# Bias rows behind V's weights and in the attention, SyncE in a fixed order until V is back, down's residual stores one per weight unit

## The chip, the cores and the metric

The kernel runs on one core of a Trainium2 chip. The metric is the device time of one execution in microseconds (us); the time of a kernel is the median over several runs. The core has five engines that work side by side, each in its own program order: PE (TensorE, matrix products), DVE (VectorE), ACT (ScalarE), POOL (GpSimd) and SP (SyncE, which here only issues transfers). Transfers (DMAs) are issued by SP and in some places by ACT; sixteen DMA engines carry them out.

## The reference, cut to what matters

The computation is a transformer encoder of two layers over 1024 tokens of 1024 features, in fp32. Each layer has a combined input projection, three groups of attention heads (A: neighbourhood attention on a grid, with a relative bias; B: a sliding window with a T5 bias and sinks; C: dense, with norms and rotary), an output projection, and a SwiGLU FFN of width 2816.

```python
def reference(x, c, w_mod, b_mod, g_attn, w_in, rpb_na, sink_sw, t5_table, gq_ax, gk_ax,
              g_group, w_o, g_ffn, w_gu, w_down, g_final):
    cond = jax.nn.silu(c)
    for l in range(DEPTH):
        mod = cond @ w_mod[l] + b_mod[l]
        sh_a, sc_a, gt_a, sh_f, sc_f, gt_f = [m[:, None, :] for m in split_cols(mod, (D,) * 6)]
        h = rms_norm(x, g_attn[l]) * (1 + sc_a) + sh_a
        proj = h @ w_in[l]
        qa, ka, va, qb, kb, vb, qc, kc, vc = split_cols(proj, IN_SPLITS)
        ya = neighborhood_attention(qa, ka, va, rpb_na[l])
        yb = sliding_window_attention(qb, kb, vb, sink_sw[l], t5_table)
        yc = axial_attention(qc, kc, vc, gq_ax[l], gk_ax[l])
        y = jnp.concatenate([rms_norm(ya, ga), rms_norm(yb, gb), rms_norm(yc, gc)], axis=-1)
        x = x + gt_a * (y @ w_o[l])
        h = rms_norm(x, g_ffn[l]) * (1 + sc_f) + sh_f
        gate, up = split_cols(h @ w_gu[l], (FFN_HIDDEN, FFN_HIDDEN))
        x = x + gt_f * ((jax.nn.silu(gate) * up) @ w_down[l])
    return rms_norm(x, g_final)
```

## The kernel before

Every fp32 operand of a product is held as two rounded halves, hi and lo, and each product is three matmuls (hi x hi, hi x lo, lo x hi) with 512 columns, accumulated in PSUM. So every weight block that arrives by DMA passes two steps before PE can use it: ACT rounds it (`whi<-wst`, `wpt<-w`, `wpt<-graw`), and DVE or POOL subtracts to get the rest (`wlo<-wst,whi`).

All instructions are issued through one helper, so the profile puts them all on line L49; they are told apart by their tiles. The helper can pin an engine: `pin(engines, True)` ties each further instruction of that engine to the one before it in program order, without a wait. Where an engine isn't pinned, a scheduler places its instructions by its own costs, and may move a transfer far from where the code has it. A transfer, whether issued by SP or by ACT, takes the next of eight completion semaphores (DMAHW0 to DMAHW7) in turn, and its issue waits until the transfer that had the same semaphore before has landed.

A layer runs through these stages, in the order of PE:

1. Token projections: a loop t = 0 to 9 over blocks of 128 tokens. It makes group C's queries and keys (norm, rotary on POOL and DVE: `cq`, `ct`; transposes `pq`, `pk`), a first part of the queries and keys of A and B (`ps_ab`, rounded to `qko` and stored to DRAM as `qkd` by SP), and at t = 8 and 9 the first V products (`ps_v`). `v_stage` at t = 4 loads V's weights as four pairs of 128 rows (tiles `wst`, `wst`, `wsv`, `wsv`, three transfers each). In layer 0 `bias_rows` at t = 3 makes the bias tables in DRAM: `skA` (two, one for each layer, each 4 x 128 copies of a row of 512 values, 1 MB, DRAM to DRAM), `rowB` (the T5 bias less its mask, 12 KB) and `skB` (six, each 128 copies of a row of `rowB`, 256 KB). The tables for group A of layer 0, `zv<-skA`, read the first skA in stage 2; layer 1 reads the second. `bz<-skB` reads skB in the attention, for group B.
2. The AB stage: the other V products (`v_proj`), then the queries and keys of A and B by columns `oc` 2 to 7 in two halves each, twelve halves of 24 matmuls (`ps_ab`). After each half ACT and DVE round the result (`qko`) and ACT issues two stores `qkd<-qko`, one half later. Beside this SP streams the adaLN weights (`wmt`), which DVE multiplies and adds up (`acc`), and loads the AB weights (`wst`).
3. The heads' attention: a stream n of pairs, 24 of C, 16 of A and 24 of B, with scores (`sC`), ACT's exponential (`pr`), transposes (`T`, `pt`) and products with V (`pv`). At n = 0 eight `v_store` write A's part of V to DRAM (`vAd<-vs`) and at n = 6 eight `v_back` bring it back in another order of rows (`vs<-vAd`), 256 KB each.
4. The output projection, then the FFN: gate and up, whose result goes to DRAM (`gpd`), and down, 77 weight units of 48 matmuls in seven products in the order 1, 2, 6, 7, 4, 5, 3, with weights `w` and activations `graw<-gpd` (one transfer for two units) loaded ahead. In layer 0, when product 4 is done, the gains and rotary tables of the next layer are loaded (`g`, `cst`), and `spill(0)` stores the finished half of the residual in eight transfers (`xd<-xb`).

SP is pinned in stage 2 and in the FFN, and unpinned in stages 1 and 3. So the vAd stores and vs loads, which the code issues in the attention, are placed by the scheduler: it has moved them up into the AB stage, among the wmt.

## Time and profile before

| what | us |
|---|---|
| median of 3 runs | 2412.68 (2412.14 to 2415.06) |
| profiled execution | 2419.0 |
| its span | 2417.2 |
| PE busy | 2343.7 (97% of the span) |
| DVE busy | 1756.8 (73%) |
| ACT busy | 1194.7 (49%) |
| POOL busy | 744.0 (31%) |

In the rows of the timeline a line gives the start and duration in us, the engine, the operation with its output and input tiles, the shape, and in brackets how long the engine stood idle before it and what it waited for. `SPq` and `ACTq` are the issues of transfers by SP and ACT; their duration is the time to issue, and with several in one row it takes in the waits between them. "DMA to landing" is the time from the issue to the arrival of the last byte. PEclk is the share of TensorE's full clock that was granted.

### The profile page before, as it was taken

The page shows a single profiled execution, that of the slowest core. Times are in us where ns is not written, and L with a number is a line of the kernel's source. Part 1 is how long each engine was busy: PE and PEld are TensorE (multiplying, and loading weights), DVE is VectorE, ACT ScalarE, POOL GpSimd, SP SyncE. Part 2 cuts the span into 40 slices and gives each one's busy share as a digit, 9 for nine tenths or more (in the row PEclk, how much of TensorE's full clock was granted, in tenths as well). Part 3 has the DMA queues.
Part 4 walks back from the last instruction along what each step waited for, and adds up shares of the span by engine and source line. Part 5 has one row for each costly group of instructions (what it writes and reads, how often), then busy time and mean ns, then how long its engine had stood idle before and what let it go on. Part 6 is the DMA issues. An engine that isn't in the chain of part 4 may idle for free.

```text
span 2417.2 us, 33362 instructions
## 1 busy us (share of the span) xinstructions
PE 2343.7 (97%) x11733; PEld 1957.8 (81%) x11733; DVE 1756.8 (73%) x2788; ACT 1194.7 (49%) x2250; POOL 744.0 (31%) x719
## 2 busy tenths in 40 slices
PE   8999999999999999999999999999999999999998
PEld 4777899888788787788787879988888888888886
DVE  5756898977967788587578579988797545447865
ACT  3421688954543333344444138897454333334443
POOL 1430345720144444300037114465004444430001
PEclk9999999999999999999999999999999999999999
DMA  8478215254245454596433861151534332329633
GB/s 264 143 235 274 71 27 133 58 178 149 92 144 179 157 182 153 158 285 191 138 110 97 282 198 32 27 161 61 196 99 160 116 101 96 121 90 298 212 129 109
DMA packets 305336, 356.95 MB, mean 148 GB/s; under 512 B 51964, under 2 KB 221788, under 8 KB 305168
## 3 DMA queue, kind: packets, MB, share of 16 engines
q1 hardware_dynamic: 283296, 342.07, 44.5%
q10 hardware_dynamic: 21504, 12.59, 2.0%
q8 instruction: 92, 1.51, 0.2%
q14 instruction: 76, 0.62, 0.1%
q0 software_dynamic: 368, 0.17, 0.0%
HBM read 269.79 MB, written 88.63 MB: 148 GB/s over the span
## 4 chain that ended last, share of the span: by engine, by line
PE 45%; DVE 5%; issue 4%; DMA 4%; ACT 3%; POOL 1%; SPq 0%; ACTq 0%; POOLq 0%; DVEq 0%
PE ps_w L49 21%; PE ps_d L49 11%; PE ps_o L49 3%; PE pv L49 2%; PE T L49 2%; PE ps_v L49 2%; PE sC L49 2%; DMA qkd<-qko 1%; DVE wpt L49 1%; ACT pr L49 1%; DMA w<-in_w_down_dram 1%; PE ps_c L49 1%; DMA cst<-const_rope_dram 1%; DMA graw<-gpd 1%; DVE xb L49 0%
## 5 line engine op out<-in xcount | busy, mean ns | idle before, releaser
L49 PE MATMUL ps_d<-wpt 128*128 128x512 f32 x1848 | 424.3, 390 | 4.0 <-ACT wpt L49 3.4
L49 PEld LDWEIGHTS ps_d<-wpt 128*128 128x128 f32 x1848 | 345.5, 188 | 78.1 <-issue 3.3
L49 POOL TENSOR_SCALAR pr<-pr,rs 128x1024 f32<-128x1024 f32 (+2 forms) x248 | 193.7, 794 | 219.3 <-DVE rs L49 190.3
L49 POOL TENSOR_TENSOR sg<-sg,u 128x512 f32<-128x512 f32 x82 | 116.5, 1421 | 353.6 <-ACT sg L49 227.8
L49 PE MATMUL pv<-pt,vs 128*128 128x256 f32 x1088 | 175.5, 296 | 17.2 <-DVE y L49 13.3
L49 DVE TENSOR_TENSOR pt<-T,pt 128x512 fp32r<-128x512 f32 x272 | 176.8, 678 | 7.4 <-ACT pt L49 7.1
L49 ACT CAST wpt<-w 128x512 fp32r<-128x512 f32 x154 | 95.9, 622 | 170.5 <-PE ps_d L49 153.1
L49 ACT CAST pt<-T 128x512 fp32r<-128x512 f32 x272 | 152.3, 585 | 40.7 <-PE T L49 38.6
L49 ACT COPY u<-ps_w 128x512 f32<-128x512 f32 x128 | 75.2, 587 | 189.9 <-PE ps_w L49 189.9
L49 POOL TENSOR_TENSOR wpt<-ws,wpt 128x512 fp32r<-128x512 f32 x80 | 110.4, 1381 | 186.2 <-ACT wpt L49 139.8
L49 DVE TENSOR_TENSOR wpt<-w,wpt 128x512 fp32r<-128x512 f32 x154 | 109.4, 710 | 79.5 <-ACT wpt L49 79.3
L49 PEld LDWEIGHTS pv<-pt,vs 128*128 128x128 f32 x1088 | 141.4, 189 | 30.0 <-DVE y L49 25.6
L49 PE MATMUL T<-identr,pr 128*128 128x128 f32 x1176 | 161.6, 273 | 0.9 <-DVE edge L49 0.4
L49 DVE SCALAR_TENSOR_TENSOR acc<-wmt,condT,acc 128x512 f32<-128x512 f32 (+1 forms) x98 | 117.2, 1204 | 47.0 <-DMA wmt<-in_w_mod_dram 46.3
L49 PEld LDWEIGHTS T<-identr,pr 128*128 128x128 f32 x1176 | 137.9, 140 | 16.1 <-issue 1.4
L49 ACT CAST wpt<-ws 128x512 fp32r<-128x512 f32 x176 | 108.1, 624 | 59.8 <-issue 28.2
L49 DVE TENSOR_TENSOR wpt<-ws,wpt 128x512 fp32r<-128x512 f32 x96 | 81.8, 861 | 62.1 <-ACT wpt L49 62.0
L49 DVE TENSOR_TENSOR wpt<-graw,wpt 128x512 fp32r<-128x512 f32 x154 | 110.3, 716 | 21.3 <-ACT wpt L49 21.1
L49 ACT CAST wpt<-graw 128x512 fp32r<-128x512 f32 x154 | 95.2, 618 | 60.0 <-DMA graw<-gpd 50.5
L49 DVE TENSOR_REDUCE rs<-sC 128x1 f32<-128x1024 f32 x88 | 107.3, 1221 | 17.8 <-PE sC L49 13.7
L49 DVE TENSOR_TENSOR ws<-wr 128x512 f32<-128x512 f32 x88 | 78.9, 899 | 54.2 <-POOL wpt L49 51.1
L49 PE MATMUL sC<-qk 128*128 128x512 f32 x384 | 108.9, 407 | 6.4 <-ACT pr L49 6.4
(300 smaller groups left out, 5945.7 us busy)
## 6 DMA issues: line engine op xcount, KB each, us to landing
wr<-in_w_gu_dram SPq DMA_DIRECT2D x92, 512.0 KB, 4.2
gpd<-sg SPq DMA_DIRECT2D x154, 256.0 KB, 4.4
graw<-gpd SPq DMA_DIRECT2D x76, 512.0 KB, 3.5
w<-in_w_down_dram SPq DMA_DIRECT2D x110, 256.0 KB, 5.1
wmt<-in_w_mod_dram SPq DMA_DIRECT2D x48, 512.0 KB, 6.1
qk<-qkd SPq DMA_DIRECT2D x44, 512.0 KB, 6.6
wst<-in_w_o_dram SPq DMA_DIRECT2D x32, 512.0 KB, 3.9
wmt<-in_w_mod_dram SPq DMA_DIRECT2D x64, 256.0 KB, 3.7
```

What stands on the lines that cost most here:

```text
L49: ins = op(*args, **kwargs)
```

## The change

Three edits, all to what SP issues. The rows of PE, DVE, ACT and POOL are the same before and after.

The first splits `bias_rows`. The store of `rowB` stays at t = 3; the copy to layer 0's skA is written behind `v_stage` at t = 4, and the copy to layer 1's skA and the six skB are written at n = 4 of the attention, in layer 0. SP's rows in stage 1, from the first stores of `qkd` to V's weights, before (skA_92 is layer 1's table, skr the rows it copies):

```order
L49 DMA qkd<-qko 512x1x64 x4
L49 DMA skA_92<-skr 512x1x512
L49 DMA rowB<-wsv 6x512
L49 DMA qkd<-qko 512x1x64 x2
L49 DMA skB<-rowB 128x512 x6
L49 DMA qkd<-qko 512x1x64 x2
L49 DMA wst<-in_w_in_dram 128x2x256
L49 DMA wst<-in_w_in_dram 128x2x128 x2
L49 DMA wst<-in_w_in_dram 128x2x256
L49 DMA wst<-in_w_in_dram 128x2x128 x2
```

and after:

```order
L49 DMA qkd<-qko 512x1x64 x5
L49 DMA rowB<-wsv 6x512
L49 DMA qkd<-qko 512x1x64 x3
L49 DMA wst<-in_w_in_dram 128x2x256
L49 DMA wst<-in_w_in_dram 128x2x128 x2
L49 DMA wst<-in_w_in_dram 128x2x256
L49 DMA wst<-in_w_in_dram 128x2x128 x2
```

skA_92 and the six skB are gone from here, and V's weights follow the eight stores directly. Layer 0's own table, skA_91, stands further up in SP's rows, at the start of stage 1, where the scheduler places it in both kernels (these rows are of after; before has the same five):

```order
L49 DMA cst<-const_rope_dram 128x128 x4
L49 DMA t_428<-in_t_table_dram 32x6
L49 DMA skA_91<-skr 512x1x512
L49 DMA wst<-in_w_in_dram 128x8x128
L49 DMA xd<-xt 128x512 x16
```

Moved in the code, it has not moved on SP.

The second keeps SP pinned from the AB stage on until `v_back` at n = 6, in both layers, so that the order of the code holds there. SP's rows in the middle of layer 0's AB stage, before:

```order
L49 DMA wmt<-in_w_mod_dram 128x1024
L49 DMA wst<-in_w_in_dram 128x8x128
L49 DMA wmt<-in_w_mod_dram 128x1024 x2
L49 DMA zAd<-zt 128x640
L49 DMA wmt<-in_w_mod_dram 128x1024
L49 DMA vs<-vAd 128x1x512
L49 DMA wst<-in_w_in_dram 128x8x128
L49 DMA vs<-vAd 128x1x512 x4
L49 DMA wmt<-in_w_mod_dram 128x1024 x3
L49 DMA vs<-vAd 128x1x512 x3
L49 DMA wst<-in_w_in_dram 128x8x128
L49 DMA wmt<-in_w_mod_dram 128x1024 x6
```

and after, from the last weights of the AB stage to the attention:

```order
L49 DMA wmt<-in_w_mod_dram 128x1024 x3
L49 DMA wst<-in_w_in_dram 128x8x128
L49 DMA wmt<-in_w_mod_dram 128x1024 x6
L49 DMA vAd<-vs 128x512 x8
L49 DMA skA_92<-skr 512x1x512
L49 DMA skB<-rowB 128x512 x6
L49 DMA vs<-vAd 128x1x512 x8
L49 DMA qk<-qkd 64x2x1024 x2
L49 DMA qk<-qkd 128x1024
L49 DMA zA<-zAd 128x640 x2
L49 DMA bz<-skB 128x384 x2
L49 DMA wst<-in_w_o_dram 128x1024 x2
```

The eight vAd stores, which stood among the wmt in rows above the ones shown, and the eight vs loads now follow the last wmt, with skA_92 and the six skB between them. Behind these come the loads of the attention (qk, zA, bz) and of the output projection. Before, zA x2, bz x2 and two loads of w_o followed the last wmt directly, and then qk.

The third replaces `spill(0)` after product 4 of down in layer 0, eight stores in one go, by one store with each of the next eight units (`at_unit`). SP's rows there (cst are rotary tables), before:

```order
L49 DMA g_10827<-in_gq_ax_dram 128x6x64
L49 DMA g_10827<-in_gk_ax_dram 128x2x64
L49 DMA cst<-const_rope_dram 128x128 x4
L49 DMA xd<-xb 128x512 x8
L49 DMA graw<-gpd 128x1024 x2
L49 DMA cst<-const_rope_dram 128x128
L49 DMA graw<-gpd 128x1024 x3
L49 DMA xd<-xb 128x512 x4
L49 DMA graw<-gpd 128x1024 x2
```

and after:

```order
L49 DMA g_10827<-in_gq_ax_dram 128x6x64
L49 DMA g_10827<-in_gk_ax_dram 128x2x64
L49 DMA cst<-const_rope_dram 128x128 x4
L49 DMA xd<-xb 128x512 x2
L49 DMA graw<-gpd 128x1024
L49 DMA xd<-xb 128x512 x2
L49 DMA cst<-const_rope_dram 128x128
L49 DMA graw<-gpd 128x1024
L49 DMA xd<-xb 128x512 x2
L49 DMA graw<-gpd 128x1024
L49 DMA xd<-xb 128x512 x2
L49 DMA graw<-gpd 128x1024 x2
```

The stores now stand in twos between the loads of graw.

The diff:

```diff
--- before.py
+++ after.py
@@ -964,9 +964,12 @@
             for i in range(2):
                 pe.matmul(ps[0:6], t5h[:, i, :], oneh, start=(i == 0), stop=(i == 1))
             dve.tensor_tensor(out=mB, in0=mB, in1=ps[0:6], op=ALU.subtract)
-            for i in range(2):
-                sp.dma_start(skA[i], bc(skr[4 * i : 4 * i + 4][:, None, :], [4, P, 512]))
             sp.dma_start(rowB, mB)
+
+        def rows_A(i):
+            sp.dma_start(skA[i], bc(skr[4 * i : 4 * i + 4][:, None, :], [4, P, 512]))
+
+        def rows_B():
             for h in range(6):
                 sp.dma_start(skB[h], bc(rowB[h][None, :], [P, 512]))
 
@@ -1021,6 +1024,8 @@
                 w = split_tile(wab.pop(0), KC, (ct, "wx", 2))
                 for kp in range(4):
                     v_stage(kp)
+                if l == 0:
+                    rows_A(0)
             if t == 6:
                 v_split_w(pool)
                 v_split_w(dve)
@@ -1196,7 +1201,7 @@
                     mod_one()
                 store = ab_split(oc, half, ps, ab)
         store(act)
-        pin((pe, act, dve, sp, pool), False)
+        pin((pe, act, dve, pool), False)
         close(ab_cm)
         close(h_cm)
         close(ps_cm)
@@ -1645,6 +1650,11 @@
             if n in (0, 6):
                 for j in range(8):
                     (v_back if n else v_store)(j)
+            if n == 4 and l == 0:
+                rows_A(1)
+                rows_B()
+            if n == 6:
+                pin((sp,), False)
             if n == 50:
                 yq = qk_tile()
             if n == 54:
@@ -2273,7 +2283,8 @@
                     cc_cm, ccp = open_pool("cc", side="right")
                     csts.clear()
                     g8 = gains_load(ccp, 1)
-                    spill(0)
+                    for n in range(KC):
+                        at_unit(u + 1 + n, lambda n=n: spill(0, (n,)))
                 beside = chain(early_half(), odd_squares())
         for _ in beside:
             pass
```

## Prediction

> **What bounds the kernel.** I read the page first, then PE's waits, then the timeline of each engine around every PE wait that lies beside moved work.

> The page's busy time by engine:

> ```profile
> PE 2343.7 (97%) x11733; PEld 1957.8 (81%) x11733; DVE 1756.8 (73%) x2788; ACT 1194.7 (49%) x2250; POOL 744.0 (31%) x719
> ```

> The waits of PE, whole run (waited in total, times, longest):

> ```profile
> PE pv L49 <- DVE y L49: 13.3, 22, 1.0
> ...
> PE ps_d L49 <- ACT wpt L49: 3.4, 2, 2.6
> ...
> PE ps_v L49 <- POOL wlo L49: 1.7, 1, 1.7
> ...
> PE ps_ab L49 <- ACT whi L49: 1.6, 1, 1.6
> ...
> PE ps_ab L49 <- DVE wlo L49: 0.8, 1, 0.8
> ```

> PE is the bound, and its program order is the same in both kernels, as are DVE's, ACT's and POOL's; SP's alone differs. So the time can move only through PE's gaps, and through the clock that a gap can cost. Of 73.5 us outside PE's busy time most is work of other places (the 22 waits for y, for one) that no moved transfer touches. The last four rows lie beside moved transfers, and so does the start of attention; each is now followed to its cause.

> **Gap 1: layer 0, V's weights.** PE, then two windows (busy of PE, PEld, DVE, ACT, POOL; PEclk, DMA share, GB/s), then SP's issues, then ACT and POOL:

> ```profile
> 132.31 0.51 PE L49 MATMUL ps_v<-wlo,hh 128*128 128x512 f32 x1 [1.70 <-POOL wlo L49]
> 132.40:136.20 3.80, 3.80 (x10) 2.99 (x11) 3.80 (x5) 3.42 (x7) 0.00 (x0) 0.55 0.41 89
> 113.00:116.30 3.30, 3.30 (x22) 2.72 (x20) 2.46 (x5) 1.07 (x5) 3.30 (x2) 1.00 0.27 94
> 103.42 0.66 SPq L49 DMA_DIRECT2D skA<-skr  x1
> 107.65 2.86 SPq L49 DMA_DIRECT2D qkd<-qko  x2
> 116.33 3.76 SPq L49 DMA_DIRECT2D skB<-rowB  x6
> 121.46 5.23 SPq L49 DMA_DIRECT2D wst<-in_w_in_dram  x6
> 128.77 1.05 ACT L49 CAST whi<-wst 128x1024 fp32r<-128x1024 f32 x1 [4.44 <-DMA wst<-in_w_in_dram]
> 116.93 3.19 POOL L49 TENSOR_TENSOR ct<-cq,cst 128x512 f32<-128x512 f32 x3
> 125.20 1.35 POOL L49 TENSOR_TENSOR ct<-ct,ct 128x512 f32<-128x512 f32 x1
> 129.90 2.36 POOL L49 TENSOR_TENSOR wlo<-wst,whi 128x1024 fp32r<-128x1024 f32 x1 [3.35 <-DMA wsv<-in_w_in_dram]
> ```

> SP stops from 110.5 to 116.33 for the rows' store, then issues six copies of 256 KB, and only at 121.46 V's weights. ACT converts them at 128.77, POOL subtracts at 129.90, PE stands 1.70 us, and afterwards runs 3.80 us at a granted clock of 0.55: ten matmuls where a full clock would do some seventeen, 0.45 x 3.80 = 1.7 us. The gap costs 3.4 us, not 1.70. [...]

> The change takes the second large copy (the skA row) and the six skB out of this place. skA's other copy stands in the same SP row before and after, so moving it in the source is worth nothing. V's weights then issue from about 110.5, and with the 7.3 us that passed from 121.46 to ACT's start the first pair is in by 118. POOL ends its ct at 126.55 and adds 2.36: wlo at 128.9, against 130.6 when PE wanted it. The second pair's buffer is freed by the POOL work that ends at 116.93, so the rest issues by some 122.5 (5.23 for six) and is in by 129.8, still ahead of PE's need of it. I take the whole 3.4 (ends 0 and 3.4), with 1.7 us to spare. A later weight load, which waits for POOL too, now stands ahead of eight stores qkd in SP's rows; it waits for that same subtraction, so the stores follow from 129 on, and what reads them back belongs to the attention (sC first at 248.66, below): nothing.

> **Gap 2: layer 0, the AB stage.** PE, a window behind, ACT, SP; then how long the stores qkd took to land in two stretches (190 to 216, and 1410 to 1440):

> ```profile
> 226.29 0.51 PE L49 MATMUL ps_ab<-hh,whi 128*128 128x512 f32 x1 [1.64 <-ACT whi L49]
> 227.55 0.50 PE L49 MATMUL ps_ab<-hh,wlo 128*128 128x512 f32 x1 [0.76 <-DVE wlo L49]
> 227.80:231.80 4.00, 4.00 (x12) 3.08 (x12) 3.86 (x7) 0.23 (x1) 0.00 (x0) 0.57 0.40 106
> 216.06 0.60 ACT L49 ACTIVATE qko<-ps_ab 128x512 fp32r<-128x512 f32 x1 [5.72 <-DMA vs<-vAd]
> 224.71 0.60 ACT L49 ACTIVATE qko<-ps_ab 128x512 fp32r<-128x512 f32 x1 [8.05 <-DMA wmt<-in_w_mod_dram]
> 196.00 4.66 SPq L49 DMA_DIRECT2D vs<-vAd  x4
> 207.05 6.25 SPq L49 DMA_DIRECT2D vs<-vAd  x3
> DMA to landing us min/median/max: 3.6/7.9/8.8
> DMA to landing us min/median/max: 3.1/3.3/6.6
> ```

> ACT is held for 5.72 and 8.05 us by transfers of SP that it doesn't use: ACT's stores and SP's transfers share eight completion semaphores, as the program's waits show, so a store can issue only when the transfer eight places earlier in that common count has landed. Sixteen transfers of 256 KB (vAd, vs) stand in that count inside the stage. Behind the late ACT, whi is late: 1.64 + 0.76 us, and 0.43 x 4.00 = 1.7 us of clock, 4.1 in all. The change moves all sixteen behind the last wmt. ACT then waits for stores and wmt alone; 3.3 us median where few others ran. I take 4.1 (ends 0 and 4.1): whi has to come 2.4 us sooner, while the two waits before it are 5.7 and 8.1.

> **Gap 3: the start of attention.** PE in layer 0 and layer 1, DVE, and ACT's last stores:

> ```profile
> 248.66 2.33 PE L49 MATMUL sC<-qk 128*128 128x512 f32 x8 [0.37 <-ACT pr L49]
> 1425.79 2.35 PE L49 MATMUL sC<-qk 128*128 128x512 f32 x8 [1.72 <-ACT pr L49]
> 1418.82 0.69 DVE L49 SCALAR_TENSOR_TENSOR qko<-ps_ab,qko 128x512 fp32r<-128x512 f32 x1 [0.63 <-ACT qko L49]
> 263.25 2.36 DVE L49 TENSOR_REDUCE rs<-sC 128x1 f32<-128x1024 f32 x2 [1.38 <-DMA qkd<-qko]
> 265.77 2.08 PE L49 MATMUL sC<-qk 128*128 128x512 f32 x4 [2.18 <-ACT pr L49]
> 258.68 1.24 ACTq L49 DMA_DIRECT2D qkd<-qko  x2
> ```

> 0.37 and 1.72 us come from a DVE that is late from the AB stage, which waits in it for ACT's qko; of these 2.1 us I take 1.5 (ends 0 and 2.1), since DVE keeps its own work there. Against it stands the new load of this place. In layer 0, behind the last wmt, SP now issues eight vAd, skA's second copy (1 MB), six skB and eight vs (256 KB each), 6.8 MB, where by SP's rows two zA and two bz stood. DVE's reduction at 263.25 can't start before the last stores of 258.68 are in, and PE waits 2.18 us for what follows it: each us by which these land later is a us of PE. What this costs no row of this place shows. Below it nothing is gained but what an earlier ACT brings. Above it the nearest row is the skA copy of 103.42: the store of 107.65 beside it took 9.1 us to land, the maximum in the next rows, where others there took 2.4.

> ```profile
> DMA to landing us min/median/max: 2.4/5.7/9.1
> ```

> 259.3 + 9.1 is 268.4, 5.2 us later than the 263.2 of before; ACT's gain in gap 2 brings the stores forward by perhaps 2 to 4, so the price lies between 0 and 3. I take 1.2, since skA itself should be nearly done by then: at the 94 GB/s of the window 113 to 116.3, 1 MB takes 11 us and ends by about 258. That window's DMA share of 0.27 is four engines of sixteen. [...]

> Layer 1 gets vAd and vs at this place without the bias rows, at 0 (ends -0.5 and 1). zA, bz, qk and w_o now stand behind these transfers in SP's order; they are first used in pairs many steps later, tens of us, so I cost that at nothing. If the cover were gone, A's first pair would be late.

> **Gap 4: down in layer 0.** PE, ACT, POOL's use of the g load that stands just ahead of the cst loads, SP, and the landing times of the cst loads:

> ```profile
> 1195.30 6.01 PE L49 MATMUL ps_d<-wpt 128*128 128x512 f32 x24 [2.65 <-ACT wpt L49]
> 1194.63 0.62 ACT L49 CAST wpt<-graw 128x512 fp32r<-128x512 f32 x1 [9.47 <-DMA graw<-gpd]
> L49 POOL TENSOR_SCALAR g<-g x1: 1172/1172/1172, 1185.8 to 1185.8; 128x384 f32<-128x384 f32 x1
> 1174.34 7.77 SPq L49 DMA_DIRECT2D cst<-const_rope_dram  x4
> 1182.15 7.42 SPq L49 DMA_DIRECT2D xd<-xb  x8
> 1189.67 1.20 SPq L49 DMA_DIRECT2D graw<-gpd  x2
> DMA to landing us min/median/max: 5.1/12.6/12.8
> ```

> The graw of the next unit stands behind eight xd stores. They issue from 1182.15 to 1189.57, each waiting for a landing eight places back (the cst loads take 12.6 us); graw issues at 1189.67 and lands about 5 us later. With two xd ahead of it instead of eight, the first graw's place waits for the g load, which POOL takes up at 1185.8 as it lands: issue at about 1185.8, landing 4.5 to 5.5 later at 1190.3 to 1191.3. PE stood from 1192.65 and ACT's row is 0.67 ahead of PE's, so it is wanted by 1192.0. So 2.65 and its follower 0.7 (the wait row's 3.4) vanish; no clock loss follows this gap, so none is counted. Ends 0 and 3.9 (small slow matmuls behind the gap); I take 3.4. What the spread stores delay is later graw, by one 256 KB store each, under landings of 4 to 5 us with a unit of some 3 us of work ahead: nothing, while two are ahead.

> **Sum.** 3.4 + 4.1 + 1.5 + 3.4 - 1.2 = 11.2 us off. The profiled execution took 2419.0 (span 2417.2), 0.26% above the median of the runs, 2412.68; its gaps I assume in the others too: 2412.68 - 11.2 = 2401.5.

> **Rivals.**
> - Stores late at the start of attention: the skA copy or what runs around it holds ACT's last stores, in layer 1 the vs loads do, through the common count. For: a store took 9.1 us beside skA. Against: that is 5.2 us at most by the nearest row, and the stores come earlier. It decides against the kernel only beyond 11.2 + 1.2 + 4.8 = 17 us of lateness. If all 6.8 MB went first at the 94 GB/s of the skA window, 72 us from 240 on, the stores would land at 312, 49 us late: 2412.7 - 12.4 + 49 = 2449. With half of that, 2425. Chance 0.07.
> - AB's gap stays, as wmt alone keeps the stores slow: the second row of gap 2 has a wait for wmt, and in the stretch 1410 to 1440 some stores took 6.6 us. Then 3.4 + 3.4 - 1.2 = 5.6: 2407. Chance 0.15.
> - Down still stalls: the slow cst loads stand ahead of graw as before, and if its place waits for one of these (landed at some 1188, by the rows), graw comes at 1193, and of 3.4 some 2.4 are gained: 2402.5; with nothing gained, 2405. Chance 0.17.
> - The void change: only order on SP moves, and all landings turn out bound by bandwidth, not by order: 2412, within 0.2%. For: DMA is slow there anyway. Against: each gap shows an engine idle for a single late transfer with idle DMA nearby (0.27). Chance 0.08.

> **How the numbers follow.** My forecast, all four gaps closing in the main, has 0.53. Its own range is 2397 to 2405: the upper ends 3.4 + 4.1 + 2.1 + 3.9 + 0.5 with the new load at 0 are 14.0, 2398.7, and less 1.5 for what the median itself may move (the runs of before reach 0.5 below and 2.4 above it); 3.4 + 4.1 + 0 + 3.4 - 3 = 7.9 is the other end, 2404.8. The rivals that keep one gap reach 2407, and with 3 us for the load 2409: range 2396 to 2410, with the void change, the slow case and a part of the tail outside. Faster by over 0.2% (4.8 us, about what a measurement can tell from no change) takes the forecast, 0.12 of AB's rival and all of down's: 0.82; within it lie the void and the rest of AB's, 0.11; slower 0.07.

> **What would show it.** Right: no PE wait over 0.5 us at ps_v near 132, clock 1.00 at 132 to 136 and 228 to 232, ACT's waits for vs gone from AB in both layers, the sC wait of layer 1 under 0.7, the ps_d wait after product 4 under 0.5. Wrong: a longer DVE wait for qkd ahead of the first rs (263.25 before, less the time won by then), a wait of PE on qk<-qkd or bz, or V's subtraction still late, now for wst.

## The result, and the profile after

The changed kernel runs in 2403.3 us (median; 2399.43 to 2405.66), the kernel before beside it in 2412.41 (2409.68 to 2415.06): a ratio of 0.9962, 95% interval 0.9952 to 0.9972, some 9.1 us less. On another chip it was 0.9971 (0.9959 to 0.9982), 6.7 us by the medians. The profiled execution took 2405.66 us, span 2403.9: 13.3 us less than the profiled execution of before. That the profiles differ by more than the medians is the main finding below.

PE's waits in the changed kernel, first over the stretch from V's weights to the start of attention:

```profile
PE sC L49 <- ACT pr L49: 3.4, 1, 3.4
PE pv L49 <- ACT pt L49: 1.7, 1, 1.7
```

and PE's rest of gap 4, over the whole run:

```profile
PE ps_d L49 <- ACT wpt L49: 0.7, 1, 0.7
```

The waits for wlo at ps_v and for whi and wlo at ps_ab are gone from this stretch; one at the start of attention (sC) has grown. Gap 1's place: SP's issues, POOL, PE, and the window behind (PEclk is the third number from the right):

```profile
109.70 8.60 SPq L49 DMA_DIRECT2D wst<-in_w_in_dram  x6
118.35 3.03 SPq L49 DMA_DIRECT2D wsv<-in_w_in_dram  x6
126.45 3.39 POOL L49 TENSOR_TENSOR wlo<-wst,whi 128x1024 fp32r<-128x1024 f32 x1
130.02 0.39 PE L49 MATMUL ps_v<-wlo,hh 128*128 128x512 f32 x1
130.00:134.00 4.00, 4.00 (x19) 3.30 (x19) 3.93 (x6) 0.75 (x3) 0.30 (x1) 1.00 0.72 188
```

V's weights issue 11.8 us sooner than before. POOL's subtraction took 3.39 us where it took 2.36, ends at 129.84, and PE's first use follows at 130.02 without a gap. The start of attention in layer 0: PE, DVE, ACT's last two stores, and SP:

```profile
251.70 0.39 PE L49 MATMUL pv<-pt,vs 128*128 128x256 f32 x1 [1.68 <-ACT pt L49]
257.57 1.20 PE L49 MATMUL sC<-qk 128*128 128x512 f32 x4 [3.36 <-ACT pr L49]
255.05 2.36 DVE L49 TENSOR_REDUCE rs<-sC 128x1 f32<-128x1024 f32 x2 [2.57 <-DMA qkd<-qko]
248.29 2.25 ACTq L49 DMA_DIRECT2D qkd<-qko  x2
222.34 10.95 SPq L49 DMA_DIRECT2D vAd<-vs  x8
233.34 1.66 SPq L49 DMA_DIRECT2D skA<-skr  x1
235.47 17.21 SPq L49 DMA_DIRECT2D skB<-rowB  x6
254.12 5.22 SPq L49 DMA_DIRECT2D vs<-vAd  x8
```

ACT's stores issue 10.4 us earlier than before (248.29 against 258.68), but DVE's reduction starts only 8.2 us earlier, and PE's wait is 3.36 us instead of 2.18. The semaphores in the trace show what holds it: the second of these two stores takes the semaphore that layer 1's skA had before it. skA, issued at 233.34, lands at 249.93; the store issues at 249.96 and lands at 254.93; DVE starts at 255.05. Down in layer 0, SP, ACT and PE:

```profile
1173.11 0.91 SPq L49 DMA_DIRECT2D xd<-xb  x2
1175.69 0.32 SPq L49 DMA_DIRECT2D graw<-gpd  x1
1180.54 0.62 ACT L49 CAST wpt<-graw 128x512 fp32r<-128x512 f32 x1 [4.95 <-DMA graw<-gpd]
1196.11 1.17 PE L49 MATMUL ps_d<-wpt 128*128 128x512 f32 x4 [0.71 <-ACT wpt L49]
```

The first graw issues behind two stores, lands about 4.9 us later, and PE doesn't wait for it. The 0.71 us of before, which I had counted as a follower of the large gap, is still there.

Where the two profiled executions part, found by the start of each matmul in both: 3.5 us at ps_v, 4.4 at ps_ab, 0.9 at the first sC, 3.3 at down's graw, 1.6 at layer 1's first sC. The start of attention in layer 0 gives 1.4 back at once and regains as much, since the half clock that followed there in the profile of before (granted clock 0.66 from 265.8 to 270.8 us) didn't come (1.00 from 257.6 to 262.6).

### The profile page after: what moved, and what is told of

Same layout as the page of the kernel before. It is cut to its first block, busy times and chain, and to the rows that moved or that the text cites. A ratio compares the mean times of both kernels' runs of the same rounds, so it can differ in the third digit from the quotient of the medians.

```text
span 2403.9 us, 33342 instructions
## 1 busy us (share of the span) xinstructions
PE 2337.2 (97%) x11733; PEld 1954.9 (81%) x11733; DVE 1756.9 (73%) x2788; ACT 1192.2 (50%) x2250; POOL 744.0 (31%) x719
## 5 line engine op out<-in xcount | busy, mean ns | idle before, releaser
L49 PE MATMUL ps_d<-wpt 128*128 128x512 f32 x1848 | 423.8, 390 | 1.1 <-ACT wpt L49 0.7
L49 PEld LDWEIGHTS ps_d<-wpt 128*128 128x128 f32 x1848 | 345.7, 188 | 74.4 <-issue 3.0
L49 POOL TENSOR_SCALAR pr<-pr,rs 128x1024 f32<-128x1024 f32 (+2 forms) x248 | 193.0, 791 | 220.8 <-DVE rs L49 196.8
L49 POOL TENSOR_TENSOR sg<-sg,u 128x512 f32<-128x512 f32 x82 | 116.6, 1422 | 354.0 <-ACT sg L49 228.4
L49 PE MATMUL pv<-pt,vs 128*128 128x256 f32 x1088 | 175.8, 296 | 17.7 <-DVE y L49 13.4
L49 DVE TENSOR_TENSOR pt<-T,pt 128x512 fp32r<-128x512 f32 x272 | 176.9, 678 | 8.3 <-ACT pt L49 8.0
L49 ACT CAST wpt<-w 128x512 fp32r<-128x512 f32 x154 | 95.7, 621 | 174.6 <-PE ps_d L49 156.1
L49 ACT CAST pt<-T 128x512 fp32r<-128x512 f32 x272 | 151.8, 584 | 40.6 <-PE T L49 38.8
L49 ACT COPY u<-ps_w 128x512 f32<-128x512 f32 x128 | 75.1, 587 | 190.1 <-PE ps_w L49 190.1
L49 POOL TENSOR_TENSOR wpt<-ws,wpt 128x512 fp32r<-128x512 f32 x80 | 110.9, 1388 | 186.5 <-ACT wpt L49 140.3
L49 DVE TENSOR_TENSOR wpt<-w,wpt 128x512 fp32r<-128x512 f32 x154 | 108.9, 707 | 79.8 <-ACT wpt L49 77.7
L49 PEld LDWEIGHTS pv<-pt,vs 128*128 128x128 f32 x1088 | 141.7, 190 | 30.8 <-DVE y L49 26.0
L49 PE MATMUL T<-identr,pr 128*128 128x128 f32 x1176 | 161.6, 273 | 0.8 <-DVE edge L49 0.4
L49 PEld LDWEIGHTS T<-identr,pr 128*128 128x128 f32 x1176 | 137.9, 140 | 16.0 <-issue 1.3
L49 DVE SCALAR_TENSOR_TENSOR acc<-wmt,condT,acc 128x512 f32<-128x512 f32 (+1 forms) x98 | 113.9, 1172 | 44.6 <-DMA wmt<-in_w_mod_dram 44.2
L49 ACT CAST wpt<-ws 128x512 fp32r<-128x512 f32 x176 | 107.8, 622 | 60.0 <-issue 28.1
L49 DVE TENSOR_TENSOR wpt<-ws,wpt 128x512 fp32r<-128x512 f32 x96 | 82.9, 872 | 62.0 <-ACT wpt L49 61.9
L49 DVE TENSOR_TENSOR wpt<-graw,wpt 128x512 fp32r<-128x512 f32 x154 | 110.1, 715 | 17.4 <-ACT wpt L49 17.4
L49 ACT CAST wpt<-graw 128x512 fp32r<-128x512 f32 x154 | 95.0, 617 | 52.9 <-DMA graw<-gpd 48.8
L49 DVE TENSOR_REDUCE rs<-sC 128x1 f32<-128x1024 f32 x88 | 107.3, 1221 | 17.7 <-PE sC L49 12.3
L49 DVE TENSOR_TENSOR ws<-wr 128x512 f32<-128x512 f32 x88 | 78.9, 899 | 53.9 <-POOL wpt L49 50.8
L49 PE MATMUL sC<-qk 128*128 128x512 f32 x384 | 107.5, 403 | 5.8 <-ACT pr L49 5.6
```

The source lines that it names most:

```text
L49: ins = op(*args, **kwargs)
```

## The experiments

**One program, four executions.** The kernel before, once more and profiled.

> The kernel before, once more, to see how executions of one program differ. Theory A (the clock drops follow the gaps): its trace has the same gaps (1.70 us at ps_v near 132, 1.64 and 0.76 at ps_ab near 226, 2.65 at ps_d near 1195) and the same half-clock stretches of 3.4 to 4 us behind the first two. Theory B (a drop is a matter of chance in when the gap falls): the gaps are the same within 0.1 us, but at least one of the drops is missing or another one is there, and the granted clock differs between executions by 0.001 to 0.002, which goes with 2 to 5 us of time. B makes the profiled execution of before, 2419.0 against a median of 2412.4, a draw with many drops, and the gain of 13.3 us between the two profiled executions against 9.1 between the medians is then no loss of a gain.

Ratio 1.000 (0.9988 to 1.0011); its executions ran from 2407.22 to 2417.92 us at a granted clock of 0.992 to 0.996, those at 0.992 at 2416.4 and 2417.9. Theory A fell. PE's waits in the stretch from V's weights to the start of attention:

```profile
PE sC L49 <- ACT pr L49: 3.2, 2, 2.2
PE pv L49 <- ACT pt L49: 1.4, 1, 1.4
PE ps_v L49 <- POOL wlo L49: 1.1, 1, 1.1
```

Gap 1 is 1.06 us and no half clock follows (granted clock 1.00 from 129.7 to 133.7); gap 2 isn't there. So the gaps differ too, more than theory B had it. Two more profiles of before:

> A third look at the kernel before, for how often PE waits in layer 0's AB stage. In three executions with this stage the wait at half 8 (ps_ab for whi) was the lateness of ACT's qko of half 5 less 10.2 us, or nothing: 11.87 gave 1.64, 13.68 (bias rows alone moved) gave 3.45, 9.07 gave none. So here: no wait where half 5 is under 10.2 us late, and the difference where it is over. If the wait comes from something else, the two numbers don't go together.

> A fourth look, with the same expectation. If the wait of the first profile was a rare draw, at most one of these two shows it; if it is the rule, both do.

They took 2413.36 and 2411.03 us. The waits for whi were absent from both, as expected where half 5 (of the twelve, counted from 0) is under 10.2 us late: it was 9.83 and 9.67 us late, from the end of PE's last matmul of the half to ACT's start on its qko. A wait for wlo of 0.6 and 0.5 us was there. In the first of the two, the wait at ps_v and the window behind it:

```profile
PE ps_v L49 <- POOL wlo L49: 1.7, 1, 1.7
130.50:134.50 4.00, 4.00 (x11) 3.18 (x12) 3.97 (x6) 3.30 (x7) 0.00 (x0) 0.58 0.44 94
```

and in the second:

```profile
PE ps_v L49 <- POOL wlo L49: 1.7, 1, 1.7
130.30:134.30 4.00, 4.00 (x17) 3.19 (x18) 3.97 (x5) 3.35 (x7) 0.00 (x0) 1.00 0.44 97
```

The same gap, to 0.04 us, is followed by eleven matmuls in 4 us at a granted clock of 0.58, or by seventeen at 1.00. Over the four profiles of before, and the two of the changed kernel (the second comes from a run further down); "yes" is a granted clock of 0.57 to 0.66 over the 4 or 5 us behind the gap, "no" one of 1.00:

| PE idle, us (half clock behind it) | first | again | third | fourth | after | after again |
|---|---|---|---|---|---|---|
| gap 1, ps_v | 1.70 (yes) | 1.06 (no) | 1.72 (yes) | 1.68 (no) | 0 | 0 |
| gap 2, ps_ab | 2.40 (yes) | 0 | 0.63 (no) | 0.47 (no) | 0 | 0 |
| first sC, layer 0 | 0.37 | 1.01 | 1.29 | 1.42 | 0 | 0 |
| sC behind the stores, layer 0 | 2.18 (yes) | 2.16 (yes) | 2.16 (no) | 2.15 (yes) | 3.36 (no) | 3.44 (no) |
| gap 4, first ps_d | 2.65 (no) | 2.54 (yes) | 2.83 (yes) | 2.63 (no) | 0 | 0 |
| first sC, layer 1 | 1.72 | 0.49 | 0.87 | 0 | 0 | 1.10 |
| sC behind the stores, layer 1 | 2.17 (yes) | 1.88 (no) | 2.19 (yes) | 2.17 (no) | 2.28 (yes) | 2.25 (no) |

**The parts alone.** The bias rows moved, with SP unpinned as before and the spill in one go:

```diff
-            for i in range(2):
-                sp.dma_start(skA[i], ...)
...
+                if l == 0:
+                    rows_A(0)
...
+            if n == 4 and l == 0:
+                rows_A(1)
+                rows_B()
```

> The bias rows moved as in the change, SP not pinned in the attention and the spill in one go as before. SP's order then has skA's second copy right behind V's weights and the six skB among the wmt late in the AB stage. If the parts add up: the gap at ps_v near 132 is gone and the AB stage is as before, -3.4 us (with the clock, -1.7 without a drop in most executions). Rival, that the bias rows only move the trouble: 1.5 MB more among the wmt make ACT's qko later in the AB stage, PE's wait there grows from 2.4 us to 4 or more, and the whole is between -1.5 and +2 us.

1.0012 (1.0001 to 1.0023): slower by some 3 us (0.2 to 5.5), the rival's case and beyond. The wait at ps_v is gone, as the part was to do, but the loss in the AB stage is larger. PE and ACT there:

```profile
221.87 0.50 PE L49 MATMUL ps_ab<-hh,whi 128*128 128x512 f32 x1 [3.45 <-ACT whi L49]
211.20 0.60 ACT L49 ACTIVATE qko<-ps_ab 128x512 fp32r<-128x512 f32 x1 [9.25 <-DMA skB<-rowB]
220.28 0.60 ACT L49 ACTIVATE qko<-ps_ab 128x512 fp32r<-128x512 f32 x1 [8.49 <-DMA vs<-vAd]
```

Without the pin the scheduler lifts skB out of the attention into the AB stage. ACT now waits 9.25 us for one. By the end of PE's half 5 ACT is 13.68 us late, and PE waits 3.45. In the first profile of before it was 11.87 and 1.64; both times the wait is the lateness less 10.23 us. In the other profiles of before and in the spill's alone, half 5 is 9.07 to 9.83 us late, under that slack, and no wait for whi follows. So gap 2 is an edge that half 5 reaches in some executions.

SP pinned alone, `pin((pe, act, dve, pool), False)` after the AB stage and `pin((sp,), False)` at n = 6:

> SP alone pinned until V is back, bias rows and spill as before. The gap at ps_v near 132 stays at 1.7 us. My reading of gaps 2 and 3: PE's waits at ps_ab near 226 vanish, ACT's waits for vs are gone from the AB stage, layer 1's sC wait (1.72) falls under 0.7, and with no bias rows at the start of attention layer 0 loses nothing there: -4 to -6 us. Rival (wmt alone keeps the stores slow): the ps_ab wait stays over 1 us and the time is within 1.5 us of before.

0.9987 (0.9977 to 0.9997), 3.1 us: less than my 4 to 6. PE's largest waits from V's weights to the start of attention:

```profile
PE sC L49 <- ACT pr L49: 2.0, 2, 1.9
PE ps_v L49 <- POOL wlo L49: 1.6, 1, 1.6
```

Half 5 is 1.31 us late, the waits at ps_ab are gone, and of those at the first sC 0.15 us is left in layer 0; what they had cost was less than the first profile showed. Down's wait is 1.43 us in this profile, at a place that this edit doesn't reach, so gap 4 scatters too. Down's stores spread alone, `at_unit` for `spill(0)`:

> Only down's stores spread, one per unit. My reading of gap 4: PE's wait of 2.65 us near 1195 is gone, a rest of at most 0.7 stays, -3.3 us; all gaps before it as in the kernel before. Rival (the slow cst and g loads are what holds graw, not the stores): PE still waits 1 us or more at that graw, and the gain is under 1.5 us.

0.9987 (0.9975 to 0.9999), 3.1 us. Its only wait in down:

```profile
PE ps_d L49 <- ACT wpt L49: 0.7, 1, 0.7
```

The rival with the slow cst loads falls: they are where they were. Both without the bias rows' move:

> The change without its bias rows: SP pinned until V is back and down's stores spread, the rows copied at t = 3 as before. If the parts of the change add up, this is the sum of the two parts alone, -4.3 - 3.2 = -7.5 us against before, and the bias rows are worth the rest to -9.1, some -1.6 us: the gap at ps_v (1.1 to 1.7 us and now and then a clock drop) less the new load of 1 to 1.4 us at the start of attention. Rival: the bias rows are worth nothing or cost, then this is at -9 or lower.

0.9974 (0.9963 to 0.9985), 6.3 us, as the two parts' 3.1 and 3.1 add up. The whole change was 9.2 and 7.0 us by its two ratios, so under the pin the bias rows would bring between 0.7 and 2.9; with 2 to 3 us to either side of each ratio, even the sign isn't shown. Alone they cost 3.

**What holds ACT in the AB stage.** The sixteen vAd and vs transfers of the kernel before, one head of four; the other three are neither stored nor brought back (the main lines of the edit):

```diff
...
-                f32(vs[:, j, 0:4, :]),
+                f32(vs[:, j, 0, :]),
...
```

> The kernel before with the sixteen vAd and vs transfers cut to one head of four, 64 KB each instead of 256 KB; the other three heads of group A's V keep the wrong order of rows. The order on SP and the turn of the semaphores stay nearly as before (two vs in front of one weight load instead of one), the bytes are a quarter. If it is the number of transfers in the common count and SP's own waiting that make ACT late, halves 3 to 7 of layer 0's AB stage stay 6 us and more late (7 to 9 in the second look at before). If it is their bytes and landing times, the lateness falls to the 0 to 3 us that the pinned order shows, and the time by the 4 us of that part.

0.9981 (0.9971 to 0.9991), 4.6 us. Half 5 is 5.76 us late, between the 9 to 12 of before and the 1.3 of the pinned order, and PE's waits at ps_ab and at the first sC of both layers are gone from its profile. ACT's two largest waits in the stage:

```profile
ACT qko L49 <- DMA qkd<-qko: 17.0, 4, 6.0
ACT qko L49 <- DMA vs<-vAd: 12.3, 2, 8.0
```

Even with vs of 64 KB ACT is held for up to 8.0 us. Bytes explain about half of the lateness; the rest would fit ACT's turn behind transfers that SP itself issues late. That there is such a turn the first profile of before shows: a vs issued at 207.05 lands at 213.57, and ACT's store, next on the same semaphore, issues at 213.59. But the count of transfers wasn't tried by itself, so its share of the lateness stays argued.

**The new load at the start of attention.** Layer 1's skA with the 128 copies outermost:

```diff
-                rows_A(1)
+                sp.dma_start(
+                    skA[1].rearrange("h p c -> p h c"),
+                    bc(skr[4:8][None, :, :], [P, 4, 512]),
+                )
```

> The change with layer 1's skA copied in another order, the 128 copies outermost instead of the four heads. If the outermost dimension of 4 keeps the copy on four engines (DMA share 0.27 and 94 GB/s while it ran alone, 11 us for its 1 MB), it now runs on sixteen: well over 94 GB/s, the store that needs its semaphore issues sooner, and the skB behind it issue over 9 us instead of 17. Of PE's 3.36 us at the start of attention up to 1.2 goes. Rival (the bytes count, not the engines): the same 3.4 us, since 6.8 MB pass there in either case.

0.9986 (0.9975 to 0.9997): most of the change's gain is lost. Two windows of the changed kernel:

```profile
232.00:238.00 6.00, 6.00 (x28) 4.99 (x27) 4.42 (x6) 4.22 (x6) 0.07 (x1) 1.00 0.82 256
238.00:244.00 6.00, 6.00 (x28) 4.93 (x27) 4.65 (x8) 0.60 (x1) 2.15 (x2) 1.00 0.69 205
```

and of this one, with PE, ACT and SP:

```profile
232.00:238.00 6.00, 6.00 (x28) 4.93 (x28) 2.67 (x4) 2.21 (x3) 0.00 (x0) 1.00 0.97 285
238.00:244.00 6.00, 5.67 (x24) 4.08 (x23) 3.83 (x8) 2.01 (x4) 2.23 (x2) 1.00 1.00 282
251.61 3.45 PE L49 MATMUL sC<-qk 128*128 128x512 f32 x8 [4.86 <-ACT wst L49]
247.86 0.60 ACT L49 ACTIVATE qko<-ps_ab 128x512 fp32r<-128x512 f32 x1 [7.86 <-DMA vs<-vAd]
231.98 8.00 SPq L49 DMA_DIRECT2D skB<-rowB  x6
242.60 5.62 SPq L49 DMA_DIRECT2D vs<-vAd  x8
```

The skB came as expected, in 8 us instead of 17; for PE's wait both cases missed. skA lands 8.4 us after its issue instead of 16.6, and so the vs loads come 11.5 us earlier: now ahead of ACT's last stores, where ACT waits 7.86 us for one. Behind the slow copy they had come after those stores. The landing of this skA is signalled in sixteen steps, that of the changed kernel in five, the last four of them 15.8 to 16.6 us after the issue; over how many engines it ran isn't shown. Here the faster copy costs 4.86 us of PE.

The rows behind V's way back, at n = 10, SP pinned until there, in two runs:

```diff
-            if n == 4 and l == 0:
-                rows_A(1)
-                rows_B()
-            if n == 6:
+            if n == 10:
+                if l == 0:
+                    rows_A(1)
+                    rows_B()
                 pin((sp,), False)
```

> The change with layer 1's skA and the six skB issued at n = 10, behind V's way back. If they hold ACT's last stores at the start of attention, the wait of DVE's first rs for qkd falls from 2.57 us to 1.4 or less, PE's sC gap behind it from 3.36 to about 2.2, and the time is 1 us under the changed kernel's. Rival (the eight vs loads, which now come earlier, hold the stores as well): the gap stays at 3 us or more and the time is the same as the changed kernel's.

> The changed kernel once more, beside the next on one chip. Ratio to before 0.996 again. The places that the change reaches look as in the first profile: no PE wait at ps_v near 130, none at ps_ab in layer 0, 3 us or more at the sC behind the last qkd stores, nothing at the graw of down but 0.7 us.

> The change with layer 1's skA and the skB at n = 10, again, now beside the changed kernel. In the first run PE's gap behind the stores fell from 3.36 to 1.55 us, but PE waited 1.24 us before the first sC, which the changed kernel doesn't. If that comes from the eight vs loads, which now come 17 us earlier, it is there again and the two kernels are the same within 1 us; if it was chance, this one is 1 to 2 us faster than the changed kernel.

0.9960 (0.9946 to 0.9974), and then 0.9958 (0.9946 to 0.9970) beside 0.9971 (0.9959 to 0.9982) for the changed kernel: 2402.69 against 2406.65 us. The place, in the changed kernel again:

```profile
253.94 2.36 DVE L49 TENSOR_REDUCE rs<-sC 128x1 f32<-128x1024 f32 x2 [2.65 <-DMA qkd<-qko]
256.45 1.20 PE L49 MATMUL sC<-qk 128*128 128x512 f32 x4 [3.44 <-ACT pr L49]
```

and with the rows later:

```profile
239.29 2.32 PE L49 MATMUL sC<-qk 128*128 128x512 f32 x8 [0.22 <-ACT pr L49]
253.80 2.35 DVE L49 TENSOR_REDUCE rs<-sC 128x1 f32<-128x1024 f32 x2 [0.77 <-DMA qkd<-qko]
256.32 1.19 PE L49 MATMUL sC<-qk 128*128 128x512 f32 x4 [1.56 <-ACT pr L49]
236.20 5.01 SPq L49 DMA_DIRECT2D vs<-vAd  x8
```

The rows did hold the stores: the wait behind them falls from 3.44 to 1.56. In the changed kernel's second profile, too, skA lands at 248.74, ACT's last store issues at 248.76 and lands at 253.81, and DVE starts at 253.94. But the vs loads come 17 us earlier and ACT is late at halves 9 and 10 (4.65 and 5.28 us), so PE gets to this wait later, and past it at 256.32 against 256.45: a gain of 0.13 here. The 1.24 us before the first sC of its first run shrank to 0.22. The two profiled executions differ by 5.5 us; some 2.3 of it comes at layer 1's ps_ab near 1288 and 1.3 at layer 1's first sC, and from 390 us up to these places SP's order is the same in both. So most of the 4 us between the medians can't be put down to the edit. The version is the fastest here; that it is faster than the changed kernel isn't shown.

## Why the prediction was right, and where it wasn't

The time came out 1.8 us above the 2401.5 foretold, inside the range, and of the sign foretold. The sum behind it was less good than that: one of its terms was several times too large, and others were moved by the same cause. That 11.2 us came as near as it did to the 9.1 measured is in part luck; on the other chip the change brought 6.7.

- **Gap 1, 3.4.** The mechanism held: the wait is gone. The issue at 109.70 was foretold at 110.5; of the 1.7 us to spare 0.2 was left, since POOL's subtraction took 3.39 and not 2.36 us and PE came 0.6 us sooner. The size didn't hold. Three of the four profiles of before have a gap of 1.7 us and one of 1.06, and the half clock follows two of the four: (1.70 + 1.06 + 1.72 + 1.68) / 4 + 1.7 / 2 = 2.4.
- **Gap 2, 4.1.** The step that failed in size. The pin takes ACT's waits for vs out of AB, as foretold, but PE's wait of 2.4 us and its half clock stand in one profile of four. By the four: (2.40 + 0 + 0.63 + 0.47) / 4 + 1.7 / 4 = 1.3. The rival that AB brings little was nearer, for another reason than it gave: the wait it left standing mostly isn't there before either.
- **Gap 3, 1.5.** The first sC waits average 1.0 us in layer 0 and 0.8 in layer 1, and both are gone after, but for 1.10 in one of two profiles of layer 1: about 1.2.
- **The new load, 1.2.** 3.40 less 2.16 is 1.2 us. DVE's reduction waits behind ACT's last stores, as written. What holds the last of these is the first rival's way, at a small price: skA through the common count. I had it nearly done by then, with an estimate of 11 us; it took 16.6, and the store issued 0.03 us after it landed. Against the pinned kernels without the rows here (1.55 to 1.89 us at this wait) the price is nearer to 1.7; the pin wins back the difference. My sum also has no half clock at this wait, which three of the four profiles of before show, 1.3 us on average, and neither of the changed kernel. In layer 1 the same wait stayed, as taken. The slower rival needed 17 us of lateness and got 1.2; the wide copy shows that its place is real, with 4.86 us through vs loads in front of the stores, which I had feared for layer 1.
- **Gap 4, 3.4.** 2.65 and the half clock behind half of the gaps, 2.7 + 0.85 = 3.5, and 3.1 measured alone. Two errors cancel: the 0.71 that I added is still there, and the half clock that I left out, since the first profile had none, follows two of four. The rival with the cst loads fell.
- **skA's first copy** stands where it stood, and no time was counted for it.

With these sizes the sum is 2.4 + 1.3 + 1.2 + 3.5 - 1.2 = 7.2, or 8.5 with the half clock that the changed kernel lacks behind the stores, beside 9.1 and 6.7 measured. The profiled execution was 0.26% above its median, and I took its gaps for those of the others; that step, in the sum, is where the 4.1 came from. The scatter of before over all runs, 2404.29 to 2421.32 us, is nearly twice the gain.

## What to carry to other kernels

Before a gap in one profile is priced, ask for its slack: a wait that is the excess over a threshold (10.2 us here) may be absent from the next execution of the same program, and the profile here, 0.26% slower than the median, held more of these than its share. What a gap cost in clock differed between executions (0.58 behind 1.72 us and 1.00 behind 1.68 at one place), so one profile doesn't show that either. Where an engine waits for its own store, look for the transfer that had the store's semaphore before: here a copy of SP held ACT's last store (landing at 249.93 us, issue at 249.96). Moving transfers without pinning their queue can put them in a worse place than before; here the same move cost some 3 us unpinned, and none that could be seen under the pin. A slow transfer ahead in a queue can shield a critical one of another engine: making it faster may let what is queued behind it in too early (4.86 us of PE here).

## What the runs showed of the hardware

A PE gap of 1.56 to 1.72 us at the same place (gap 1) was followed by a granted clock of 0.57 to 0.60 over the next 4 us in four of seven executions (1.65, 1.66, 1.70, 1.72) and by 1.00 in the other three (1.56, 1.68, 1.68), and the 3.36 and 3.44 us gaps of the changed kernel by 1.00 over 5 us. So the length of a gap alone doesn't decide it. In the first profile of before the stretch behind gap 1 lasts 3.41 us at 0.50, which is 1.7 us of clock.

```profile
129.25:132.67 3.42, 1.55 (x10) 0.93 (x9) 1.21 (x1) 2.85 (x4) 2.36 (x1) 1.00 0.76 221
132.67:136.08 3.41, 3.41 (x10) 2.64 (x9) 3.41 (x4) 3.03 (x7) 0.00 (x0) 0.50 0.42 90
252.45:255.87 3.42, 1.72 (x14) 1.40 (x12) 0.85 (x2) 0.59 (x1) 0.00 (x0) 1.00 0.83 212
255.87:259.28 3.41, 1.71 (x11) 1.49 (x12) 3.21 (x5) 2.83 (x6) 0.00 (x0) 1.00 0.96 295
259.28:262.69 3.41, 3.41 (x24) 3.02 (x23) 3.41 (x6) 3.06 (x5) 2.24 (x2) 1.00 0.96 289
```

In the first, 1.87 us of idle PE fall into one window, and the next is at half clock. In the second, the longer gap is shared by two windows, with 1.70 us in each, and no half clock follows. Between 81 and 2386 us these two traces have seven full-clock windows with 1.87 to 2.59 us of idle PE, and half clock follows each; it follows none of the eight with 1.33 to 1.72 us, and none of the other 1328, with 1.19 us or less. Two executions make no bound: half clock also came behind a gap 1 of 1.65 and of 1.66 us (granted clock 0.58 with SP pinned and the spill spread, 0.60 with the small vs), and what sets these two apart stays open. That the changed kernel lost no clock to its longest gap I put down to luck: in its first profile the gap fell across two windows; where it fell in the second isn't shown.
